# Splitting 128 tokens per partition into five tiles of two pieces, with six weight transfers on the store queue

## The chip, the cores and the metric

The kernel runs on one core of a Trainium2 chip. The metric is the device time of one execution in microseconds. A core has engines that run side by side, each with its own queue of instructions: VectorE (DVE in the profile), ScalarE (ACT), GpSimd (POOL), SyncE (SP) and TensorE, which has no work here. Transfers between the chip's main memory (HBM) and the on-chip memory (SBUF, 128 partitions) are issued by SP or ACT and carried out by 16 DMA engines.

## The reference

Every token is a row of 512 numbers and has two expert weights. The output holds each token's row twice, once times each weight; the expert indices are an input that the result does not use.

```python
batch, seq, hidden, n_experts = 16, 1024, 512, 8
k = 2
x_expanded = x[:, :, np.newaxis, :].repeat(k, axis=2)
weights = expert_weights[..., np.newaxis]
return (x_expanded * weights).astype(np.float32)
```

There are 16,384 tokens: 33.55 MB are read and 67.11 MB written, in float32.

## The kernel before

The tokens are laid over the 128 partitions, so each partition has 128 of them ("128 tokens" below means 128 per partition). They are worked through in five tiles of 25 and a rest of 3 (`groups`, `LAST`). In a tile, partition p holds 25 consecutive tokens, so that one partition's row of a load is up to 25 x 2 KB long and of a store twice that.

*Loads.* `load(i)` issues a tile's load from ACT's queue into one of two buffers of `x_pool`. The first tile comes as 9 and 16 tokens (`FIRST`). Tiles 0 and 1 are loaded ahead; after that the load of tile i + 2 is issued when tile i has been multiplied. With tile 2 the three left-over tokens are loaded into `z_tile`; a one-element copy (L76) into it ties that load to a point in ScalarE's order.

*Weights.* Three transfers on SP's queue, issued inside the first load: tile 0's weights (L97), those of tiles 1 to 4 in one strided transfer (L99), and those of the rest (L106). SP's queue also carries all stores, so these stand ahead of the first store.

*Multiplication.* `fill` gives VectorE the first `v` tokens of a piece, in operations of up to four tokens (`CH`; 4 tokens are 128x4096 elements out), and ScalarE the others, one operation for each token and weight (128x512, L119). For tiles 0 and 1 a piece has 9, 9, 9 or 8 tokens on VectorE and 4 or 3 (then 4 and 4) on ScalarE; from tile 2 on VectorE does all (`SHARES`).

*Stores.* The results go into one buffer, `o_ring`, of 25 tokens. A tile is cut into pieces at fixed places: 13 and 12 tokens in tiles 0 and 1, 9, 8 and 8 in tiles 2 to 4. Each piece is stored from SP as soon as it is filled (L154), and its place can be filled again when its store has landed. The 3-token rest is the fourteenth and last store. In the texts below 0A, 0B are the pieces of tile 0, and so on.

What sets the order is the order in which the program issues work to each engine's queue, and the waits that the framework derives from the buffers: an operation waits for the landing of what it reads and of the store that last read the place that it writes.

Of the kernel before, what the change touches and what calls it, by code (L numbers as in the profile page):

```python
# [1 line left out]

# [4 lines left out]


@with_exitstack
def kernel(  # L10
    ctx: ExitStack,
    tc: tile.TileContext,
    x: bass.AP,
    expert_indices: bass.AP,
    expert_weights: bass.AP,
    out: bass.AP,
):
    nc = tc.nc

    batch, seq, hidden = x.shape  # L20
    k = expert_weights.shape[-1]
    P = nc.NUM_PARTITIONS
    ntok = batch * seq
    assert ntok % P == 0
    A_TOTAL = ntok // P

    f32 = mybir.dt.float32
    row = k * hidden
    CH = 4


    groups = [25, 25, 25, 25, 25]
    TX = max(groups)
    LAST = 3
    FIRST = [9, 16]
    SHARES = [[9, 9], [9, 8], [9, 8, 8]]
    assert sum(groups) + LAST == A_TOTAL

    xf = x.rearrange("b s h -> (b s) h")
    of = out.rearrange("b s k h -> (b s) (k h)")  # L40
    wf = expert_weights.rearrange("b s k -> (b s) k")

    w_pool = ctx.enter_context(tc.tile_pool(name="w_pool", bufs=1))
    x_pool = ctx.enter_context(tc.tile_pool(name="x_pool", bufs=2))
    o_pool = ctx.enter_context(tc.tile_pool(name="o_pool", bufs=1))

    w_tile = w_pool.tile([P, A_TOTAL * k], f32)
    o_ring = o_pool.tile([P, TX * row], f32)

    def rows(of_all, done, T):  # L50
        return of_all[done * P : (done + T) * P, :].rearrange(
            "(p a) n -> p (a n)", a=T
        )


    if LAST:
        z_pool = ctx.enter_context(tc.tile_pool(name="z_pool", bufs=1))
        z_tile = z_pool.tile([P, LAST * hidden], f32)

    tiles = []  # L60
    done = 0
    for n in groups:
        tiles.append((done, n))
        done += n

    loaded = []

    def load(i):
        if i >= len(tiles):
            return  # L70
        done, n = tiles[i]
        x_tile = x_pool.tile([P, TX * hidden], f32)
        src = rows(xf, done, n)
        steps = FIRST if i == 0 else [n]
        if i == 2 and LAST:
            nc.scalar.copy(out=z_tile[:, :1], in_=o_ring[:, TX * row - 1 :])  # L76
        for e, step in enumerate(steps):
            at = sum(steps[:e])
            nc.scalar.dma_start(  # L79
                out=x_tile[:, at * hidden : (at + step) * hidden],  # L80
                in_=src[:, at * hidden : (at + step) * hidden],
            )
            if i == 0 and e == 0:
                for g in range(3):
                    weights(g)
        if i == 2 and LAST:
            nc.scalar.dma_start(out=z_tile, in_=rows(xf, A_TOTAL - LAST, LAST))
        loaded.append(x_tile)


    T0 = groups[0]
    G = len([n for n in groups[1:] if n == T0])
    head = (1 + G) * T0

    def weights(e):
        if e == 0:
            nc.sync.dma_start(out=w_tile[:, : T0 * k], in_=rows(wf, 0, T0))  # L97
        elif e == 1:
            nc.sync.dma_start(  # L99
                out=w_tile[:, T0 * k : head * k].rearrange("p (g n) -> p g n", g=G),  # L100
                in_=wf[T0 * P : head * P, :].rearrange(
                    "(g p a) n -> p g (a n)", g=G, p=P
                ),
            )
        else:
            nc.sync.dma_start(  # L106
                out=w_tile[:, head * k :], in_=rows(wf, head, A_TOTAL - head)
            )

    def product(engine, o_tile, t, x_in, c, m):  # L110

        o = t * row
        if engine is not None:
            for e in range(m * k):
                out_e = o_tile[:, o + e * hidden : o + (e + 1) * hidden]
                in_e = x_in[:, e // k * hidden : (e // k + 1) * hidden]
                w_e = w_tile[:, c + e : c + e + 1]
                if engine is nc.scalar or engine is nc.any and (c + e) % 3 == 2:
                    nc.scalar.mul(out=out_e, in_=in_e, mul=w_e)  # L119
                else:  # L120
                    nc.vector.tensor_scalar(
                        out=out_e,
                        in0=in_e,
                        scalar1=w_e,
                        scalar2=None,
                        op0=mybir.AluOpType.mult,
                    )
            return
        nc.vector.tensor_tensor(  # L129
            out=o_tile[:, o : o + m * row].rearrange(  # L130
                "p (t k h) -> p t k h", t=m, k=k
            ),
            in0=x_in[:, : m * hidden]
            .rearrange("p (t h) -> p t h", t=m)
            .unsqueeze(2)
            .to_broadcast([P, m, k, hidden]),
            in1=w_tile[:, c : c + m * k]
            .rearrange("p (t k) -> p t k", t=m)
            .unsqueeze(3)
            .to_broadcast([P, m, k, hidden]),  # L140
            op=mybir.AluOpType.mult,
        )

    def fill(o_tile, x_in, c, m, v):
        for t in range(0, v, CH):
            u = min(t + CH, v)
            product(None, o_tile, t, x_in[:, t * hidden : u * hidden], c + t * k, u - t)
        product(nc.scalar, o_tile, v, x_in[:, v * hidden :], c + v * k, m - v)

    def emit(src, dst, c, cuts, shares):  # L150
        for at, to, v in zip(cuts, cuts[1:], shares):
            o_tile = o_ring[:, at * row : to * row]
            fill(o_tile, src[:, at * hidden : to * hidden], c + at * k, to - at, v)
            nc.sync.dma_start(out=dst[:, at * row : to * row], in_=o_tile)  # L154

    for i in range(2):
        load(i)
    for i, (done, n) in enumerate(tiles):
        cuts = [0, 13, n] if i < 2 else [0, 9, 17, n]
        emit(loaded[i], rows(of, done, n), done * k, cuts, SHARES[min(i, 2)])  # L160
        load(i + 2)
    emit(
        z_tile,
        rows(of, A_TOTAL - LAST, LAST),
        (A_TOTAL - LAST) * k,
        [0, LAST],
        [LAST],
    )

# [1 line left out]
_INS = ['x', 'expert_indices', 'expert_weights']  # L171
_OUTS = [((16, 1024, 2, 512), 'float32')]


# [23 lines left out]
```

## Time and profile before

| what | value |
|---|---|
| median of 3 runs | 241.03 us (239.64 to 241.2) |
| profiled execution | 239.66 us |
| its span in the profile | 237.9 us |
| VectorE busy | 123.8 us (52%) |
| ScalarE busy | 20.2 us (8%) |
| moved by DMA | 100.80 MB, mean 424 GB/s |

The span runs from the first instruction to the last end that the profiler recorded; the device time of the same execution is 1.8 us longer. The DMA rows of the profile give the busy share of the 16 DMA engines in slices of the span. "Landing" is the time from the issue of a transfer to its completion. SPq and ACTq are the instructions by which SP and ACT issue transfers; queue q1 carries what SP issues and q10 what ACT issues.

### The profile page before, as it was taken

Reading aid. Unit: us, or ns where it says so; the run is one execution under the profiler, and the core shown is the slowest. Engines: PE = TensorE matmul, PEld = TensorE weight load, DVE = VectorE, ACT = ScalarE, POOL = GpSimd, SP = SyncE. Lnnn points to the kernel's source line nnn. Section 1 sums busy time; section 2 is a strip of 40 time slices with the busy share of each in tenths; the row PEclk is TensorE's granted clock in tenths of the full one; section 3 lists DMA queues with packets and bytes.
Section 4 is the critical chain, followed back from the end, with each engine's and each line's share of the span. In section 5 each row is a group of like instructions: output and inputs, shape, how many; then the busy total and the mean of one; then the engine's idle time right before and its main releaser. Section 6 shows DMA issues by size and latency. Waiting matters only on the chain.

```text
span 237.9 us, 167 instructions
## 1 busy us (share of the span) xinstructions
DVE 123.8 (52%) x33; ACT 20.2 (8%) x32; POOL 0.2 (0%) x4
## 2 busy tenths in 40 slices
DVE  0499800000059293089505999493096999865000
ACT  0008900000052160000000000000000000000000
POOL 0000000000000000000000000000000000000000
DMA  7999999999999999999999999899999999999996
GB/s 259 450 422 467 467 433 415 415 391 450 439 397 397 417 430 438 496 446 407 403 419 426 484 419 474 364 452 452 439 409 430 413 435 436 477 398 441 441 441 265
DMA packets 3840, 100.80 MB, mean 424 GB/s; under 512 B 1152, under 2 KB 1152, under 8 KB 1280
## 3 DMA queue, kind: packets, MB, share of 16 engines
q1 hardware_dynamic: 2832, 67.24, 65.7%
q10 hardware_dynamic: 1008, 33.55, 33.2%
HBM read 33.69 MB, written 67.11 MB: 424 GB/s over the span
## 4 chain that ended last, share of the span: by engine, by line
DMA 68%; DVE 18%; ACT 3%; issue 2%; ACTq 0%; DVEq 0%; SPq 0%
DMA out_dram<-o_ring 60%; DVE o_ring L129 18%; DMA x_tile<-in_x_dram 7%; ACT o_ring L119 2%; ACT L119 1%; ACTq L79 0%; DVEq L129 0%; SPq L154 0%; ACTq L119 0%
## 5 line engine op out<-in xcount | busy, mean ns | idle before, releaser
L129 DVE TENSOR_TENSOR o_ring<-x_tile,w_tile 128x4096 f32<-128x4096 f32 (+1 forms) x32 | 120.4, 3820 | 91.6 <-DMA out_dram<-o_ring 69.8
L119 ACT ACTIVATE o_ring<-x_tile,w_tile 128x512 f32<-128x512 f32 x30 | 18.7, 708 | 48.1 <-DMA out_dram<-o_ring 48.0
L129 DVE TENSOR_TENSOR o_ring<-z_tile,w_tile 128x3072 f32<-128x3072 f32 x1 | 3.4, 3360 | 2.1 <-DMA out_dram<-o_ring 2.1
L119 ACT ACT_TABLE_LOAD x1 | 1.3, 1283 | 19.0 <-DMA x_tile<-in_x_dram 19.0
L76 ACT COPY z_tile<-o_ring 128x1 f32<-128x1 f32 x1 | 0.2, 191 | 0.0
L182 POOL MEMSET const-bfloat16-1.0<- 128x1 bf16 x1 | 0.1, 102 | 0.0
L182 POOL MEMSET const-uint8-127<- 128x1 uint8 x1 | 0.1, 102 | 0.0
L182 POOL MEMSET const-float32-0.0<- 128x1 f32 x1 | 0.1, 99 | 0.2 <-issue 0.2
L182 POOL MEMSET const-float32-1.0<- 128x1 f32 x1 | 0.1, 99 | 0.0
## 6 DMA issues: line engine op xcount, KB each, us to landing
x_tile<-in_x_dram ACTq DMA_DIRECT2D x4, 6400.0 KB, 30.5
out_dram<-o_ring SPq DMA_DIRECT2D x6, 4096.0 KB, 21.5
out_dram<-o_ring SPq DMA_DIRECT2D x3, 4608.0 KB, 26.8
out_dram<-o_ring SPq DMA_DIRECT2D x2, 6656.0 KB, 33.1
out_dram<-o_ring SPq DMA_DIRECT2D x2, 6144.0 KB, 44.8
x_tile<-in_x_dram ACTq DMA_DIRECT2D x1, 4096.0 KB, 17.8
x_tile<-in_x_dram ACTq DMA_DIRECT2D x1, 2304.0 KB, 8.3
out_dram<-o_ring SPq DMA_DIRECT2D x1, 1536.0 KB, 19.5
```

The lines of the kernel that those rows point to most:

```text
L76: nc.scalar.copy(out=z_tile[:, :1], in_=o_ring[:, TX * row - 1 :])
L119: nc.scalar.mul(out=out_e, in_=in_e, mul=w_e)
L129: nc.vector.tensor_tensor(out=o_tile[:, o : o + m * row].rearrange("p (t k h) -> p t k h", t=m, k=k), in0=x_in[:, : m * hidden] .rearrange ...
L182: nc = _bacc.Bacc("TRN2", target_bir_lowering=False, num_devices=1)
```

## The change

The 128 tokens become five tiles of 26, 25, 26, 25 and 26 with no rest, so `z_tile`, its load, its copy and its store are gone. Each tile has two pieces, cut at 13 tokens; the ring holds two halves of 13. There are 10 stores, of 13 tokens or, in the 25-token tiles' second piece, of 12. The two x buffers are written out as `x_even` and `x_odd`. The first tile is loaded as 9 and 17 tokens, the third as 23 and 3. The weights come in six transfers on SP: one for each of the first four tiles and two for the last, cut at 13 tokens. VectorE takes 9 tokens of each piece of tile 0 and 10 of each piece after it, in operations of 4, 4 and 1 or 2 tokens; ScalarE takes the remaining 4, 3 or 2 tokens in every tile.

In the built program, ScalarE has 16 products, then the two loads of tile 2, then 10 products of tile 1 and 2 of tile 2, the load of tile 3, and so on. The load of tile 1 waits for the landing of the first load, and the 3-token load for the landing of the fourth weight transfer.

```diff
-    groups = [25, 25, 25, 25, 25]
-    TX = max(groups)
-    LAST = 3
-    FIRST = [9, 16]
-    SHARES = [[9, 9], [9, 8], [9, 8, 8]]
-    assert sum(groups) + LAST == A_TOTAL
+    CH = 4
+    groups = [26, 25, 26, 25, 26]
+    HALF = 13
+    FIRST = 9
+    SHORT = 3
+    assert sum(groups) == A_TOTAL
...
-    o_ring = o_pool.tile([P, TX * row], f32)
+    x_even = x_pool.tile([P, groups[0] * hidden], f32)
+    x_odd = x_pool.tile([P, groups[1] * hidden], f32)
+    o_ring = o_pool.tile([P, 2 * HALF * row], f32)
...
+    def load(i, at=0, to=None):
+        if i < len(tiles):
+            part = slice(at * hidden, (to or tiles[i][1]) * hidden)
+            nc.scalar.dma_start(out=x_of(i)[:, part], in_=rows(xf, *tiles[i])[:, part])
+
+    def weights(i, *cuts):
         done, n = tiles[i]
+        for at, to in zip((0, *cuts), (*cuts, n)):
+            nc.sync.dma_start(
+                out=w_tile[:, (done + at) * k : (done + to) * k],
+                in_=rows(wf, done, n)[:, at * k : to * k],
             )
...
+    load(0, 0, FIRST)
+    for i in range(len(tiles) - 1):
+        weights(i)
+    weights(len(tiles) - 1, HALF)
+    load(0, FIRST)
+    load(1)
+    for i, (done, n) in enumerate(tiles):
+        src, dst = x_of(i), rows(of, done, n)
+        for at, to in ((0, HALF), (HALF, n)):
             o_tile = o_ring[:, at * row : to * row]
+            fill(
+                o_tile,
+                src[:, at * hidden : to * hidden],
+                (done + at) * k,
+                to - at,
+                10 if i else 9,
+            )
             nc.sync.dma_start(out=dst[:, at * row : to * row], in_=o_tile)
-    for i in range(2):
-        load(i)
-    for i, (done, n) in enumerate(tiles):
-        cuts = [0, 13, n] if i < 2 else [0, 9, 17, n]
-        emit(loaded[i], rows(of, done, n), done * k, cuts, SHARES[min(i, 2)])
-        load(i + 2)
-    emit(
-        z_tile,
-        rows(of, A_TOTAL - LAST, LAST),
-        (A_TOTAL - LAST) * k,
-        [0, LAST],
-        [LAST],
-    )
+        if i == 0:
+            load(2, 0, groups[2] - SHORT)
+            load(2, groups[2] - SHORT)
+        else:
+            load(i + 2)
```

More of the change, by code (lines that the diff above doesn't have):

```diff
@@ L43 @@
     w_pool = ctx.enter_context(tc.tile_pool(name="w_pool", bufs=1))
-    x_pool = ctx.enter_context(tc.tile_pool(name="x_pool", bufs=2))
+    x_pool = ctx.enter_context(tc.tile_pool(name="x_pool", bufs=1))
     o_pool = ctx.enter_context(tc.tile_pool(name="o_pool", bufs=1))
     w_tile = w_pool.tile([P, A_TOTAL * k], f32)
-    o_ring = o_pool.tile([P, TX * row], f32)
+    x_even = x_pool.tile([P, groups[0] * hidden], f32)
+    x_odd = x_pool.tile([P, groups[1] * hidden], f32)
+    o_ring = o_pool.tile([P, 2 * HALF * row], f32)
     def rows(of_all, done, T):
@@ L53, in rows @@
         )
-    if LAST:
-        z_pool = ctx.enter_context(tc.tile_pool(name="z_pool", bufs=1))
-        z_tile = z_pool.tile([P, LAST * hidden], f32)
     tiles = []
@@ L64 @@
         done += n
[L66 to L70, printed above, removed]
-        done, n = tiles[i]
[L72 to L81, printed above, removed]
-            )
[L83 to L88, printed above, removed]
@@ L91 @@
[L91 to L103, printed above, removed]
-            )
[L105 to L142, printed above, removed]
@@ new lines, in x_of @@
+    def x_of(i):
+        return (x_odd if i % 2 else x_even)[:, : tiles[i][1] * hidden]
+    def load(i, at=0, to=None):
[3 more added lines that the diff above has]
+    def weights(i, *cuts):
+        done, n = tiles[i]
+        for at, to in zip((0, *cuts), (*cuts, n)):
+            nc.sync.dma_start(
+                out=w_tile[:, (done + at) * k : (done + to) * k],
+                in_=rows(wf, done, n)[:, at * k : to * k],
+            )
@@ L146, in fill @@
             u = min(t + CH, v)
[L147 to L151, printed above, removed]
-            o_tile = o_ring[:, at * row : to * row]
-            fill(o_tile, src[:, at * hidden : to * hidden], c + at * k, to - at, v)
-            nc.sync.dma_start(out=dst[:, at * row : to * row], in_=o_tile)
@@ L156 @@
-    for i in range(2):
-        load(i)
-    for i, (done, n) in enumerate(tiles):
-        cuts = [0, 13, n] if i < 2 else [0, 9, 17, n]
-        emit(loaded[i], rows(of, done, n), done * k, cuts, SHARES[min(i, 2)])
-        load(i + 2)
-    emit(
-        z_tile,
-        rows(of, A_TOTAL - LAST, LAST),
-        (A_TOTAL - LAST) * k,
-        [0, LAST],
-        [LAST],
-    )
+            nc.vector.tensor_tensor(
+                out=o_tile[:, t * row : u * row].rearrange(
+                    "p (t k h) -> p t k h", t=u - t, k=k
+                ),
+                in0=x_in[:, t * hidden : u * hidden]
+                .rearrange("p (t h) -> p t h", t=u - t)
+                .unsqueeze(2)
+                .to_broadcast([P, u - t, k, hidden]),
+                in1=w_tile[:, c + t * k : c + u * k]
+                .rearrange("p (t k) -> p t k", t=u - t)
+                .unsqueeze(3)
+                .to_broadcast([P, u - t, k, hidden]),
+                op=mybir.AluOpType.mult,
+            )
@@ new lines, in fill @@
+        for e in range(v * k, m * k):
+            nc.scalar.mul(
+                out=o_tile[:, e * hidden : (e + 1) * hidden],
+                in_=x_in[:, e // k * hidden : (e // k + 1) * hidden],
+                mul=w_tile[:, c + e : c + e + 1],
+            )
+    load(0, 0, FIRST)
[7 more added lines that the diff above has]
+        for at, to in ((0, HALF), (HALF, n)):
+            o_tile = o_ring[:, at * row : to * row]
+            fill(
[4 more added lines that the diff above has]
+                10 if i else 9,
+            )
+            nc.sync.dma_start(out=dst[:, at * row : to * row], in_=o_tile)
+        if i == 0:
[3 more added lines that the diff above has]
+            load(i + 2)
```

## The prediction

> **What bounds the kernel now.** I read the page first, then busy time by stretches of the span, then the timeline, the chain of waits, the groups by shape and the transfers.
>
> ```profile
> span 237.9 us, 167 instructions
> DVE 123.8 (52%) x33; ACT 20.2 (8%) x32; POOL 0.2 (0%) x4
> DMA  7999999999999999999999999899999999999996
> DMA packets 3840, 100.80 MB, mean 424 GB/s; under 512 B 1152, under 2 KB 1152, under 8 KB 1280
> ```
>
> VectorE works half the span and ScalarE a twelfth; the DMA engines have a 9 in every slice but the first, the last and one 8. So the end is set by 100.80 MB passing through them, which the change leaves as it is: every token is still read once and written twice. The stretches show what is lost (time, three engines, clock, DMA share, GB/s; a packet seems to be booked where it starts, so a short stretch can pass 1.00 and the next falls short):
>
> ```profile
> 0.00:2.00 2.00, 0.00 (x0) 0.00 (x0) 0.20 (x4) 1.00 0.35 51
> 6.00:48.00 42.00, 19.77 (x6) 10.16 (x16) 0.00 (x0) 1.00 1.01 434
> 48.00:50.00 2.00, 0.00 (x0) 0.00 (x0) 0.00 (x0) 1.00 0.86 225
> 50.00:52.00 2.00, 0.00 (x0) 0.00 (x0) 0.00 (x0) 1.00 1.50 590
> 52.00:90.00 38.00, 17.60 (x5) 10.02 (x16) 0.00 (x0) 1.00 1.00 435
> 180.00:233.00 53.00, 32.45 (x9) 0.00 (x0) 0.00 (x0) 1.00 1.00 432
> 233.00:237.90 4.90, 0.00 (x0) 0.00 (x0) 0.00 (x0) 1.00 0.65 278
> ```
>
> I take 434 GB/s as the rate: 100.80 MB are 232.3 us of it, so of the 237.9 us some 5.6 are lost. The last 4.9 us move 1.36 MB, 3.1 us' worth: 1.8 lost. The first 2 us move 0.1 MB: 1.8 lost, with more in the ramp behind. Around 49 us there is a dip: 225 GB/s for 2 us lacks 1.0 us, of which the next row's 590 gives some back by its booking. Start and end stay; the dip may change. An edit can therefore gain about 1 us, and it can lose wherever it lets the DMA engines run dry. The question for each part is whether it does.
>
> **The change part by part.** The profiled execution took 239.66 us, 1.8 over its span; the sum goes against that. The runs shown are 239.64, 241.03 and 241.2, so with the profiled one two lie near 239.65 and two near 241.1; the mean of the four is 240.38, which is 0.72 above the profiled one.
>
> *Six weight transfers instead of three.*
>
> ```profile
> 0.72 0.37 SPq L97 DMA_DIRECT2D w_tile<-in_expert_weights_dram  x1
> 1.15 0.43 SPq L99 DMA_DIRECT2D w_tile<-in_expert_weights_dram  x1
> q1 hardware_dynamic: 376, 0.07, 3.3%
> x_tile<-in_x_dram ACTq DMA_DIRECT2D x1, 6400.0 KB, 32.6
> w_tile<-in_expert_weights_dram SPq DMA_DIRECT2D x1, 25.0 KB, 5.5
> w_tile<-in_expert_weights_dram SPq DMA_DIRECT2D x1, 3.0 KB, 50.5
> ```
>
> The last four rows are of the transfers' view for 0 to 20 us. Three more issues by 0.43 us keep SP until 3.4 us; its next work, the first store, was issued at 25.3. A transfer of 3 KB takes 50.5 us to land while the DMA engines move 434 GB/s, so the small rows wait their turn beside the loads and displace next to nothing. They are 768 rows before (128 x 1, x 4, x 1) and 768 after (6 x 128). Cost 0. Without the cover of the loads the three issues would cost 1.3 us, the upper bound; the lower is 0, as no row is saved.
>
> The Trainium skill ("DMA: Bandwidth & Descriptors", "Anatomy of one DMA") gives a fixed cost of about 2.0 us per transfer, and its "Rules for kernel authors" say that under 64 KB one pays mostly overhead; all six transfers here are below that. By it three more would add an estimated 6 us (245.7 us) if they stood on the path. The same section says that most of this cost is the wait for the last byte's receipt, which other transfers can overlap; the 434 GB/s beside a 50.5 us landing agree with that, so it stays out of the sum.
>
> *First loads, order on ScalarE.*
>
> ```profile
> 18.97 1.28 ACT L119 ACT_TABLE_LOAD   x1 [18.97 <-DMA x_tile<-in_x_dram]
> 20.27 8.68 ACT L119 ACTIVATE o_ring<-x_tile,w_tile 128x512 f32<-128x512 f32 x14
> 29.05 0.34 ACTq L79 DMA_DIRECT2D x_tile<-in_x_dram  x1
> ```
>
> Tile 0 has 26 tokens, so its second load (17 tokens) lands 0.6 us later (0.262 MB), and ScalarE has 16 products of 0.62 us instead of 14. The third tile's load is issued at 18.97 + 0.6 + 1.28 + 9.92 = 30.8 us, not 29.05. Load 1 landed at 1.6 + 32.6 = 34.2, then 34.8: the load queue has 4.0 us in hand, before 5.2. In the built program load 1 also waits for the very first load to land (VectorE starts on that at 9.05 us); the 17 tokens, issued ahead of it, occupy the engines until about 19. The 3-token load waits for the fourth weight transfer's landing; behind it on ScalarE stand only products of tile 1, which wait for store 0A until 67 us anyway. Cost 0. If the load queue did run dry, store 0A, issued at about 26, would fill in: order, not time.
>
> *The loads ahead of the first store.* It carries 77 tokens of loads instead of 78. The old 3-token load lies in the dip, where its 6 KB rows meet the last small weight rows; the new 3-token load has the same 6 KB rows and meets weight rows of 104 B. I take the dip as unchanged; bounds -1.0 (gone) to +1.0 (doubled).
>
> *Two pieces of the ring instead of three.* This is the part that could hurt: one half is stored while the other is filled, and no third piece waits in the queue. How long a fill takes:
>
> ```profile
> 25.30 42.41 DMA out_dram<-o_ring
> 67.83 9.91 DVE o_ring L129 x3
> 77.80 13.27 DMA out_dram<-o_ring
> 82.23 5.01 ACT L119 ACTIVATE o_ring<-x_tile,w_tile 128x512 f32<-128x512 f32 x8 [9.40 <-DMA out_dram<-o_ring]
> L129 DVE TENSOR_TENSOR o_ring<-x_tile,w_tile 128x1024 f32<-128x1024 f32 x6 | 7.3, 1218 | 0.0
> L129 DVE TENSOR_TENSOR o_ring<-z_tile,w_tile 128x3072 f32<-128x3072 f32 x1 | 3.4, 3360 | 2.1 <-DMA out_dram<-o_ring 2.1
> 81.00:83.00 2.00, 0.70 (x1) 0.77 (x2) 0.00 (x0) 1.00 0.99 426
> ```
>
> Store 0A lands at 67.72 and 1A is issued at 77.80: 10.08 us with 9 tokens on VectorE. After, 10 tokens: the last operation has 2048 elements, which the trace does not show; between 1218 and 3360 ns I take the midpoint, 2.29 us, so 1.07 more and 11.15 us. ScalarE's at most 6 products (4.3 us by the 8.68 for 14) lie beside it. Store 0B lands at 82.23, when ScalarE goes on: 14.51 us after 0A, as 6.29 MB at 434 GB/s should. So store 1A was issued 4.43 us before its predecessor landed, and the row of 81 to 83 us has 0.99 of the engines busy: 4.43 us are enough. How few would do is bounded below by the start: the first issue at 0.72 has bytes moving before 2.0 us, so about 1.3.
>
> After, the half in flight is 13 tokens, 15.7 us, against a fill of 11.15: 4.55 us in hand, at four hand-overs with no queue behind them (1A, 2B with load 4, 3B, 4B). One is tighter: store 3B has 12 tokens, 14.5 us, so 4A is issued 3.35 us before it lands, 1.1 less than was tested. Its cost lies between 0 (if 1.3 us are enough) and 1.1 (if it takes all of 4.43). The middle, 2.9, is below 3.35: I take 0.
>
> As landing times: 0A 67.1, 0B 82.8, then 1A, 1B and load 3 (19.66 MB) by 128, 2A, 2B and load 4 (20.45 MB) by 175, 3A 190.9, 3B 205.4, 4A 221.1, 4B 236.8. The loads land long before their tiles come (load 4 by 175, its first fill at 191). The end is where it was.
>
> *Ten stores instead of fourteen.* 512 fewer rows of data, 13 tokens each and not 3 to 13, and 64 fewer completions: 576 small steps, 36 per engine. From above a step costs what a small packet takes in the row of queue 1 (3.3% of 20 us on 16 engines over 376 packets): 28 ns, so 1.0 us. From below 0; 435 and 432 GB/s with large and with small store rows lean to a gain, but lie within the booking's noise. I take -0.3.
>
> Sum: 239.66 + 0 + 0 + 0 + 0 - 0.3 = 239.36 us for an execution like the profiled one, and with the 0.72 by which executions lie above it on the mean, **240.1 us**: no change within about 1% (2.4 us), which is what a measurement of this kernel can tell from none.
>
> **The rivals.**
> *The hand-overs run dry (slower).* If a store must be issued L us before its predecessor lands, the ring loses 4 x (L - 4.55) + (L - 3.35) us, counting positive terms. It decides from L = 5.1: then 4.0 us, 244.1 with the 0.72. For it: two pieces instead of three, and the longest landing of a store is 53.2 us in a crowded queue. Against it: no loss at 4.43. Only if the fill is also slower than I work out does it come about.
>
> ```profile
> out_dram<-o_ring SPq DMA_DIRECT2D x1, 6144.0 KB, 53.2
> ```
>
> *Small rows are dear (faster).* If a packet costs the 28 ns and the dip goes, because the new 3-token load is issued late and runs beside store rows of 53 KB, the gain is 1.0 + 1.0: 237.7 for the profiled kind, 1.4% below the median. For it: the dip stands just where 6 KB and small rows meet. Against: as many small rows are left, and 590 GB/s follows the dip.
>
> *The weight transfers come onto the path.* 1.3 us, 241.4: for it, the fourth weight transfer now releases a load; against, its landing is needed by no operation before 67 us.
>
> *The change does not hold the first store back.* The small rows could be through the queue early, with store 0A mixing with the third load. That moves landings, not bytes: still 240.1.
>
> **How the numbers follow.** Hand-overs 0.09, small rows 0.12, weights 0.05, no holding back 0.06, the forecast 0.68. Faster by over 1% is the second rival and 0.02 of the forecast, for executions that stay near 239.4: 0.14. Slower by over 1% is the first: 0.09. Within 1%: 0.77. The range goes down to 239.36 - 0.9 = 238.5 (most of the dip or of the packets) and up to 241.2 + 1.1 = 242.3 (the slower execution with the tight hand-over's full price).
>
> **What would show it.** In the changed kernel's profile: 9s in all DMA slices but the ends; 10 tokens on VectorE in 11.1 us from landing to store issue; store 0A landing near 67 us, 4A issued near 202; load 3 issued near 94 (before 91.1). Stretches under 420 GB/s at 204 to 206 us would mean that the two-piece ring runs dry, and a bare gap between 31 and 36 us that the third load comes late. A DMA digit below 9 in the middle, or a longer last stretch, makes the forecast wrong.

## The result, and the profile after

The changed kernel takes 242.19 us (median of 6 runs, 241.76 to 243.91), the kernel before 239.92 us beside it (6 runs). The ratio is 1.0104, with a 95% interval of 1.0071 to 1.0137: slower by 1%. The forecast was "no change", 240.1 us. The profiled execution took 241.89 us. Medians here and below count every run, while a ratio leaves out runs more than 1.5% above the fastest of their kernel.

From the page of the changed kernel (span, busy time, DMA slices, GB/s by slice, queues):

```profile
span 240.1 us, 193 instructions
...
DVE 107.5 (45%) x30; ACT 39.0 (16%) x61; POOL 0.2 (0%) x4
...
DMA  7999999999999999999999999999999999999993
GB/s 269 446 425 435 453 451 393 392 404 426 426 452 426 444 452 452 419 420 407 437 477 433 426 435 427 426 426 426 426 426 435 439 459 426 425 426 426 426 426 151
...
q14 instruction: 1, 0.01, 0.0%
```

The middle is as full as forecast: 9s throughout. The span is 2.2 us longer, and the only slice that looks worse is the last one, a 3 where the kernel before has a 6. A row is new: queue 14 moved one packet of 8 KB behind the start, a fetch of instructions.

The end of the changed kernel by stretches, followed by two stretches of 0.04 us, each so short that a single packet begins in it. The columns are the stretch and its length in us, the busy time of DVE, ACT and POOL, the clock, the DMA share (of the packets that begin in the stretch) and GB/s; share x 16 engines x 0.04 us is then the time of that one packet:

```profile
234.00:236.00 2.00, 0.00 (x0) 0.00 (x0) 0.00 (x0) 1.00 0.99 426
236.00:237.00 1.00, 0.00 (x0) 0.00 (x0) 0.00 (x0) 1.00 0.13 53
237.00:240.10 3.10, 0.00 (x0) 0.00 (x0) 0.00 (x0) 1.00 0.00 0
...
144.98:145.02 0.04, 0.00 (x0) 0.00 (x0) 0.00 (x0) 1.00 3.07 1331
146.38:146.42 0.04, 0.04 (x1) 0.04 (x1) 0.00 (x0) 1.00 5.32 1331
```

From 236 to 237 us 53 GB/s begin: exactly one row of 53,248 B, on one DMA engine. By the trace's packets it begins at 236.93 and ends at 238.89, while the other 15 engines end between 236.83 and 237.17. So this kernel ends with one late engine. The two short stretches show where most of its delay comes from: the first row of load 4 takes 3.07 x 0.64 = 1.97 us on an ordinary engine and 5.32 x 0.64 = 3.40 us on the late one.

I call *spread* how far the slowest of the 16 DMA engines ends a store behind their mean, worked out from the completion packets. In the kernel before it is 0.27 us at store 0A and 0.31 at the end. In the changed kernel it is 0.31 when the first load lands, 0.72 behind the second, 1.13 at store 0A, and 2.37 behind load 4. Without its late engine it would have ended some 0.4 us behind the kernel before. Followed row by row, the late engine is the one that was last at store 0A, and it works without a gap from there to the end. So its 2.2 us are about 0.9 us from the first 68 us (1.13 less 0.27) and 1.4 us from that one row of load 4.

What happens at load 4, in the timeline of the changed kernel (start, length, engine; in brackets the idle time before and what ended it):

```profile
129.12 2.56 ACT L96 ACTIVATE o_ring<-x_even,w_tile 128x512 f32<-128x512 f32 x4 [23.91 <-DMA out_dram<-o_ring]
129.19 10.96 DVE L81 TENSOR_TENSOR o_ring<-x_even,w_tile 128x4096 f32<-128x4096 f32 x3 [16.77 <-DMA out_dram<-o_ring]
...
140.24 0.35 ACTq L68 DMA_DIRECT2D x_even<-in_x_dram  x1
146.29 3.78 ACT L96 ACTIVATE o_ring<-x_odd,w_tile 128x512 f32<-128x512 f32 x6 [14.62 <-DMA out_dram<-o_ring]
...
193.44 10.96 DVE L81 TENSOR_TENSOR o_ring<-x_even,w_tile 128x4096 f32<-128x4096 f32 x3 [4.77 <-DMA out_dram<-o_ring]
...
204.46 14.83 SPq L119 DMA_DIRECT2D out_dram<-o_ring  x2
```

Store 1B lands at 129.1, the fill of 2B takes 11 us, and at 140.2 store 2B and load 4 are issued together. The completions of store 2A, which is in flight, go out 2.6 to 4.2 us later on 15 engines and 5.7 us later on one, 3.3 on the mean. In the kernel before this *lead* was 12.4 us at load 4, where a store of 8 tokens, issued 8.7 us before the load, was still in flight, and 9.8 at load 3. In the changed kernel the lead is 3.2 us at load 3 too; there the rows are too long by only 0.05 us per engine. The last two rows show the price further on: store 3A lands on the late engine, so 4A is filled from 193.44 and issued at 204.46, not near 202. Fifteen engines stand idle for some 0.4 us before it; the late one does not.

### The profile page after: what moved, and what is told of

Same layout as the page of the kernel before. It is cut to its first block, busy times and chain, and to the rows that moved or that the text cites. A ratio compares the mean times of both kernels' runs of the same rounds, so it can differ in the third digit from the quotient of the medians.

```text
span 240.1 us, 193 instructions
## 1 busy us (share of the span) xinstructions
DVE 107.5 (45%) x30; ACT 39.0 (16%) x61; POOL 0.2 (0%) x4
## 4 chain that ended last, share of the span: by engine, by line
DMA 69%; DVE 18%; issue 2%; DVEq 2%; ACT 1%; ACTq 0%; SPq 0%
DMA out_dram<-o_ring 61%; DVE o_ring L81 18%; DMA x_even<-in_x_dram 8%; DVEq L149 2%; ACT o_ring L96 1%; ACTq L68 0%; DVEq L81 0%; SPq L119 0%
## 5 line engine op out<-in xcount | busy, mean ns | idle before, releaser
L81 DVE TENSOR_TENSOR o_ring<-x_even,w_tile 128x4096 f32<-128x4096 f32 (+2 forms) x18 | 63.6, 3590 | 41.6 <-DMA out_dram<-o_ring 31.7
L81 DVE TENSOR_TENSOR o_ring<-x_odd,w_tile 128x4096 f32<-128x4096 f32 (+1 forms) x12 | 43.8, 3709 | 69.8 <-DMA out_dram<-o_ring 63.6
L96 ACT ACTIVATE o_ring<-x_even,w_tile 128x512 f32<-128x512 f32 x40 | 25.2, 709 | 60.5 <-DMA out_dram<-o_ring 60.5
L96 ACT ACTIVATE o_ring<-x_odd,w_tile 128x512 f32<-128x512 f32 x20 | 12.7, 709 | 91.1 <-DMA out_dram<-o_ring 91.1
## 6 DMA issues: line engine op xcount, KB each, us to landing
x_even<-in_x_dram ACTq DMA_DIRECT2D x1, 4352.0 KB, 18.6
```

The costliest lines, as they stand in the source:

```text
L81: nc.vector.tensor_tensor(out=o_tile[:, t * row : u * row].rearrange("p (t k h) -> p t k h", t=u - t, k=k), in0=x_in[:, t * hidden : u * h ...
L96: nc.scalar.mul(out=o_tile[:, e * hidden : (e + 1) * hidden], in_=x_in[:, e // k * hidden : (e // k + 1) * hidden], mul=w_tile[:, c + e : ...
```

## The experiments

Times stand against the kernel before on the same chip; the ratio has its 95% interval.

**Fetch of instructions or hand-overs?** The kernel before, with 34 small operations on ScalarE:

```diff
+    spare = w_pool.tile([P, 64], f32)
...
+        if i in (1, 2):
+            for e in range(17):
+                at = i * 17 + e
+                nc.scalar.copy(out=spare[:, at : at + 1], in_=w_tile[:, e : e + 1])
```

> The kernel before with 34 more one-element copies on ScalarE (0.2 us each, into a spare tile, while ScalarE has nothing to do), so that ScalarE executes 84 profiled instructions instead of 50, as many as in the changed kernel. Theory (one DMA engine is held up by a fetch of instructions in mid-run, because ScalarE has more of them): the queue of instruction fetches shows one 8 KB packet behind the start, one DMA engine ends 1.2 to 1.4 us behind the others, span 239.2, 1.3 us over the kernel before (ratio 1.005). Rival (the two-piece ring's hand-overs are the loss, and the fetch is harmless): the fetch may appear, but the span stays at 237.9 (ratio 1.000).

Measured: 239.78 us, ratio 1.0001 (0.9989 to 1.0013). The fetch is there, at 77.5 us, and holds one engine for 0.31 us; the spread at the end is 0.24 us. The fetch comes with ScalarE's number of instructions and costs nothing here. My first theory fell.

The changed kernel, with fewer products on ScalarE:

```diff
+    ON_DVE = [[9, 9], [12, 12], [13, 12], [13, 12], [10, 12]]
-                10 if i else 9,
+                ON_DVE[i][at // HALF],
```

> The changed kernel with 28 products on ScalarE instead of 60 (VectorE takes 12 or 13 tokens of the pieces of tiles 1 to 3 and of 4B), so that ScalarE executes about 52 profiled instructions; ring, loads, weights and stores are unchanged. Theory (fetch): no 8 KB fetch in mid-run, the slowest DMA engine ends 1.1 instead of 2.4 us behind the mean, span 238.7 to 238.9, 1.2 us under the changed kernel (240.6 us). Rival (hand-overs): fills are up to 2.2 us longer, so the ring runs dry more and it is slower than the changed kernel, 243 us or more.

Measured: 244.85 us, 1.0207 (1.0193 to 1.022), as the rival had it. There is no fetch. Load 4 is issued at 144.33, when store 2A has 0.6 us left. The stretch from 2 to 10 us behind that issue:

```profile
146.33:154.33 8.00, 7.30 (x2) 0.00 (x0) 0.00 (x0) 1.00 0.93 346
```

A share of 0.93 with 346 GB/s: the engines are busy and yet move a fifth less. In the packets all 16 first rows of load 4 take 2.1 to 4.1 us instead of 1.97, and most first rows of the store 2.1 to 3.1. So this is not idleness alone; rows are slow. Behind load 3, where the lead is 1.4 us, rows are too long by another 1.2 us per engine. Idle time adds 1.1 us per engine over the run.

**Parts of the change alone.** The kernel before with six weight transfers:

```diff
-                for g in range(3):
+                for g in range(6):
                     weights(g)
...
+        at, n = tiles[e] if e < len(tiles) else (A_TOTAL - LAST, LAST)
+        nc.sync.dma_start(out=w_tile[:, at * k : (at + n) * k], in_=rows(wf, at, n))
```

> The kernel before with the weights in six transfers (one for each of the five tiles, one for the rest) instead of three; all else as before. If six transfers on the store queue throw the DMA engines out of step at the start (0.4 us in the changed kernel by 19 us), the span grows by 0.4 us to 238.3 (ratio 1.002). Rival (the second load's size or the wait of the third load does it): 237.9, ratio 1.000.

Measured: 239.89 us, 1.0006 (0.9998 to 1.0015). Six transfers cost at most 0.15%. Load 1 now waits for the first load, and the 3-token load is issued at 41.5 us: the waits of the changed kernel are all there, without harm.

The changed kernel with the third tile loaded whole:

```diff
-        if i == 0:
-            load(2, 0, groups[2] - SHORT)
-            load(2, groups[2] - SHORT)
-        else:
-            load(i + 2)
+        load(i + 2)
```

> The changed kernel with the third tile loaded whole (26 tokens) instead of as 23 and 3. Theory (the 6 KB rows beside the small weight rows cost the dip at 48 to 52 us and 0.4 us of spread between the DMA engines): no dip, 0.4 to 1.2 us less than the changed kernel, 240.7 to 241.5 us; the fetch stays. Rival (the dip belongs to the small weight rows themselves, or hidden): 241.9, as the changed kernel.

Measured: 244.17 us, 1.012 (1.0077 to 1.0163): not faster at all. The expectation failed. Its profiled execution took 247.65 us, over 3 us above the median, so no profile shows a usual execution.

The changed kernel again:

> The changed kernel itself, once more, timed and profiled beside the three below. If the slow first row of load 4 on the one DMA engine that comes to it last (3.40 us instead of 1.97 at 146.4 us) is the rule, it stands again in this profile, and that engine ends 1.9 us behind the mean; if it was an accident of one execution, the span is 238 to 239 us here.

Measured: 241.83 us, 1.0061 (1.0039 to 1.0082), runs from 240.2 to 245.4. The slow row stands again in the profile (1.53 us too long, on the engine that comes last), with a spread of 1.09 us at store 0A and 1.84 at the end. Both profiles of this kernel have it, but the total varies from run to run far more than that of the kernel before (239.4 to 240.2).

The changed kernel with three pieces in tiles 2 to 4:

```diff
-        for at, to in ((0, HALF), (HALF, n)):
+        cuts = [0, HALF, n] if i < 2 else [0, 9, 17, n]
+        for at, to in zip(cuts, cuts[1:]):
...
-                10 if i else 9,
+                (10 if i else 9) if i < 2 else to - at,
```

> The changed kernel with tiles 2 to 4 cut as before, at 9 and 17 tokens, all on VectorE; loads, weights and tiles 0 and 1 stay. Theory Ring (with two pieces a load and a store are issued together with less than two store rows per engine left ahead of them, and the engine that comes to the load last pays): about 2 us less than the changed kernel, 240.2. Rival Start (the DMA engines get 0.8 us out of step by 52 us and stay so): 241.0 or more, 0.5 us of spread above that of the kernel before at the end.

Measured: 242.48 us, 1.0094 (1.0059 to 1.0129): no cure. In the profile the 3-token rows of one engine fall between the rows of the first two stores and end at 84 us instead of 52; its spread is 2.58 us by 127 us. Load 4 has a lead of 5.9 us here and still rows that are too long by 0.58 us per engine.

The kernel before with two pieces everywhere:

```diff
-    SHARES = [[9, 9], [9, 8], [9, 8, 8]]
+    SHARES = [[9, 9], [9, 8], [10, 10]]
...
-        cuts = [0, 13, n] if i < 2 else [0, 9, 17, n]
+        cuts = [0, 13, n]
```

> The kernel before with all tiles cut in two (13 and 12 tokens, 10 on VectorE and 3 or 2 on ScalarE from tile 2 on); loads, weights and the 3-token rest stay. Theory Ring: 1 to 2.5 us over the kernel before, with slow first rows of load 4. Rival Start: as before, 239.8, since nothing is changed ahead of 128 us.

Measured: 239.81 us, 1.0014 (0.9995 to 1.0033). Two pieces alone cost nothing that shows; theory Ring in that form fell. The lead at load 4 is 5.6 us here.

The changed kernel with the fetch moved forward:

```diff
+    spare = w_pool.tile([P, 64], f32)
...
             load(2, groups[2] - SHORT)
+            for e in range(30):
+                nc.scalar.copy(out=spare[:, e : e + 1], in_=w_tile[:, e : e + 1])
```

> The changed kernel with 30 one-element copies on ScalarE behind the two loads of tile 2 (at about 41 us, while ScalarE is idle), so that the 8 KB fetch of instructions falls before 90 us and not on the start of load 4 at 147 us. If the fetch at that moment is what holds up the slow row, the row is 1.97 us and the time 240.5 us; if not, 242 us as the changed kernel.

Measured: 241.15 us, 1.0049 (1.0031 to 1.0068), against 1.0061 for the changed kernel on the same chip: the intervals overlap. The fetch lies at 72 us, and the profile has no slow row, but the spread was small too (0.52 us at store 0A) and the lead 4.6 us, and the profiled execution took 240.15 us, 1.0 below the median. Inconclusive on the row, and no cure for the time.

**Tile sizes.** The changed kernel with 25-token tiles, and with one tile of 26 (the edit is the list of groups; the small last tile is stored in one piece):

```diff
-    groups = [26, 25, 26, 25, 26]
+    groups = [25, 25, 25, 25, 25, 3]   # then [26, 25, 25, 25, 25, 2], [25, 25, 26, 25, 25, 2], [25, 25, 25, 25, 26, 2]
```

> The changed kernel with tiles of 25, 25, 25, 25, 25 and 3 tokens instead of 26, 25, 26, 25, 26 (third one loaded as 22 and 3, weights in six transfers, two pieces of 13 and 12, the 3-token tile loaded when tile 3 is read and stored last). Theory Size (tiles of 26 tokens put the DMA engines out of step or slow the first rows of their loads; the ring, the six weight transfers and the waits are harmless, as the kernel before with each of them alone showed): 239.8 to 240.2 us, ratio 1.000 to 1.002. Rival Split (the 3-token load cut out of a tile, 6 KB rows 50 KB apart, does it): 241 us or more.

> As the kernel with tiles of 25 and a small last one, but the first tile has 26 tokens (loaded as 9 and 17) and the last 2. Theory Size, if the first tile decides: spread of the DMA engines over the mean of 0.7 us or more by 19 us and 241 us; if another tile does: as the kernel with tiles of 25.

> As the kernel with tiles of 25 and a small last one, but the third tile has 26 tokens (loaded as 23 and 3) and the last 2. If this tile decides: 241 us, with spread that grows at 47 to 52 us; if not: as the kernel with tiles of 25.

> As the kernel with tiles of 25 and a small last one, but the fifth tile has 26 tokens and the last 2. If load 4 with its 53 KB rows decides (the row of 3.40 us in the changed kernel): 241 us, with such a row near 146 us; if not: as the kernel with tiles of 25.

Measured: 243.38 us and 1.0138 (1.0099 to 1.0177); 241.19 and 1.0058 (1.0036 to 1.008); 242.29 and 1.0109 (1.0091 to 1.0127); 242.57 and 1.0126 (1.0107 to 1.0145). Tiles of 25 are no cure by themselves, so theory Size fell as the whole story, and the other three cannot single out a tile. The profile of the first shows something else, in the stretch from 2 to 10 us behind load 4:

```profile
139.23:147.23 8.00, 3.75 (x1) 3.79 (x6) 0.00 (x0) 1.00 0.99 378
```

Again rows are slow, with a lead of 4.0 us.

**The lead.** I then worked out, for load 4 of each trace, how long the store in flight still lasted on the mean of the engines, and by how much all rows that began in the next 12 us were too long, per engine:

| kernel | lead, us | rows too long, us per engine |
|---|---|---|
| before | 12.4 | 0.00 |
| changed, three pieces | 5.9 | 0.58 |
| before, two pieces | 5.6 | 0.03 |
| changed, early fetch | 4.6 | 0.01 |
| changed, tiles of 25, third of 26 | 4.2 | 0.96 |
| changed, tiles of 25 | 4.0 | 0.91 |
| changed | 3.3 | 0.11 (1.44 on one engine) |
| changed, load 3 | 3.2 | 0.05 |
| changed, tiles of 25, fifth of 26 | 2.8 | 0.77 |
| changed, fewer on ScalarE | 0.6 | 1.62 |

The lead orders the rows only roughly: 5.9 us did not save the kernel with three pieces, and load 3 of the changed kernel got by with 3.2. Three more runs test it, and a fourth the dip near 49 us. The changed kernel with shorter fills:

```diff
-                10 if i else 9,
+                8 if i else 9,
```

> The changed kernel with 8 instead of 10 tokens on VectorE in the pieces of tiles 1 to 4 (ScalarE 5 or 4): a fill takes 9.1 us instead of 11.3. Theory Lead (a load that is issued together with a store slows its and the store's first rows when the store in flight ends less than some 4.5 us after the issue): the lead at load 4 grows from 3.3 to 5 us or more, no slow first row, no idle time near 205 us, span 238 to 238.5, 240.0 to 240.3 us. Rival (the fetch of instructions or the spread from the start decide): 241.5 to 242.5, as the changed kernel.

Measured: 240.63 us, 1.0049 (1.0027 to 1.0071). The lead is 7.8 us, the rows are too long by 0.06, no idle time at 205 us, span 238.7. Its page, and then its timeline on ScalarE:

```profile
span 238.7 us, 215 instructions
...
DMA  7999999999999999999999999999999999999994
```

```profile
128.73 5.01 ACT L96 ACTIVATE o_ring<-x_even,w_tile 128x512 f32<-128x512 f32 x8 [19.54 <-DMA out_dram<-o_ring]
137.65 0.35 ACTq L68 DMA_DIRECT2D x_even<-in_x_dram  x1
148.29 6.24 ACT L96 ACTIVATE o_ring<-x_odd,w_tile 128x512 f32<-128x512 f32 x10 [14.55 <-DMA out_dram<-o_ring]
```

From landing (128.73) to issue (137.65) it is 9 us instead of 11, and the store in flight lands at 148.29, 10.6 us behind the issue. Hardly a slow row and no idle time are left in this profile, and the median is 0.3 us above the expected range. By the times alone the gain is not certain: the interval reaches into those of the changed kernel (1.0039 to 1.0082 and 1.0071 to 1.0137), which did not run beside it.

The changed kernel with loads 3 and 4 held back:

```diff
+            if 1 < i < len(tiles) - 1 and at == 0:
+                nc.scalar.copy(out=x_of(i + 1)[:, :1], in_=o_tile[:, HALF * row - 1 :])
+                load(i + 1)
         if i == 0:
...
-        else:
-            load(i + 2)
```

> The changed kernel with loads 3 and 4 held back by a one-element copy until the first piece of the tile before is filled, so that each is issued alone, some 10 us ahead of the end of the store in flight; the fills stay at 11.3 us. Theory Lead: no slow first rows, 240.0 to 240.6 us (the tight hand-over to 4A may stay). Rival (length of the fills, whatever is issued with the stores): 241.5 to 242.5.

Measured: 240.65 us, 1.004 (1.0021 to 1.006); load 4 is issued alone at 148.3, 18.6 us ahead of the end of the store in flight, and the rows are too long by 0.01. The fills are as long as in the changed kernel, so in this execution their length alone makes no row slow; that points to how little is left in flight when the load is issued. It is not settled: the profiled execution took 240.04 us, 0.6 below the median, and the interval overlaps the lower one of the changed kernel.

The kernel before with two pieces and longer fills:

```diff
-    SHARES = [[9, 9], [9, 8], [9, 8, 8]]
+    SHARES = [[9, 9], [9, 8], [12, 12]]
...
-        cuts = [0, 13, n] if i < 2 else [0, 9, 17, n]
+        cuts = [0, 13, n]
```

> The kernel before with all tiles cut in two, as in the earlier run, but 12 tokens on VectorE in the pieces of tiles 2 to 4, so that a fill takes 13.3 us instead of 11.1 and the lead at load 4 falls by 2.2 us, to 2 to 3.4. Theory Lead: slow first rows of load 4, 0.8 to 1.5 us per engine, 241 us or more, though fetch, start and loads are those of the kernel before. Rival (start or tile sizes): 239.8 to 240.3.

Measured: 242.81 us, 1.0118 (1.01 to 1.0136), where the same kernel with short fills had 1.0014. The lead is 1.8 us and the rows are too long by 1.08 us. From 2 to 10 us behind its load 4:

```profile
142.72:150.72 8.00, 7.45 (x2) 1.33 (x2) 0.00 (x0) 1.00 0.93 358
...
187.00:189.00 2.00, 1.91 (x1) 0.00 (x0) 0.00 (x0) 1.00 0.31 133
```

So a loss of this size can be made in the kernel before, with its start, weights and tiles untouched. The slow rows are the smaller part of it. The longer fills also leave the engines idle ahead of stores 3B and 4A, at 188 and 204 us (the second row shows the former), by the packets 1.0 us per engine each time. These 2.1 us are hand-overs that run dry.

The kernel before with the 3-token load moved behind load 4:

```diff
-        if i == 2 and LAST:
+        if i == 4 and LAST:
```

> The kernel before with its 3-token load issued behind load 4 instead of behind load 2, so that no 6 KB rows meet small weight rows. If the dip at 48 to 51 us belongs to that meeting: 0.6 to 0.8 us less than the kernel before, ratio 0.997. If it is of the weight rows themselves: 1.000. Store 0A may start to mix with the weights; that costs nothing by the prediction's steps.

Measured: 239.94 us, 1.0012 (1.0001 to 1.0022). No gain: the 6 KB rows are gone from the dip, but now the last rows of load 2 take 0.83 us per engine too long at 46 to 49 us. In both kernels the loss sits where the small weight rows run out, beside whichever load is there.

**What is left over.** Both cures together, and the fast fill with tiles of 25:

```diff
-    groups = [26, 25, 26, 25, 26]
+    groups = [25, 25, 25, 25, 25, 3]
...
-                10 if i else 9,
+                min(to - at, 8 if i else 9),
```

> Tiles of 25, 25, 25, 25, 25 and 3 tokens in two pieces, as in the earlier run with them (1.0138), but with 8 instead of 10 tokens on VectorE from tile 1 on. Theory Lead: the lead grows by some 2 us, the slow rows go, 239.8 to 240.4 us. If what is left over in the changed kernel with the fast fill (0.4 to 0.5%) belongs to the tiles of 26 tokens, this one comes to 239.8 to 240.0 (ratio 1.000 to 1.001); if it belongs to the 3-token load cut out of a tile, to 240.5.

> The changed kernel with both cures, 8 tokens on VectorE and loads 3 and 4 held back. If the 0.4 to 0.5% left over with each cure alone is still of the lead, the ratio goes to 1.000 to 1.002; if it stems from the first 52 us (the spread of the DMA engines there), it stays at 1.003 to 1.005.

Measured: with tiles of 25 and the fast fill 239.8 us, 1.0003 (0.9994 to 1.0012). Both cures with tiles of 26: 240.65 us, 1.0034 (1.0022 to 1.0046). The page of the former, and its timeline on ScalarE:

```profile
span 237.9 us, 214 instructions
...
DMA  7999989899999999999999999999999999999996
```

```profile
134.81 0.35 ACTq L68 DMA_DIRECT2D x_even<-in_x_dram  x1
145.32 5.01 ACT L96 ACTIVATE o_ring<-x_odd,w_tile 128x512 f32<-128x512 f32 x8 [14.41 <-DMA out_dram<-o_ring]
```

Load 4 goes out at 134.81, and the store in flight is landed at 145.32 on the slowest engine, 10.5 us behind it, against 6.05 in the changed kernel (140.24 to 146.29). The last slice is a 6 again, and the span that of the kernel before, with six weight transfers, a cut-out 3-token load, two pieces and the fetch all in place. The loss has two parts, then. With tiles of 25, the fills alone decide between 1.0138 and 1.0003. With the fast fill, the tiles alone decide between 1.0049 (three of 26) and 1.0003 (25 and a small last one). Both cures with tiles of 26 leave 1.0034, and in that profile it is spread: the last store lands at 236.76 on the mean of the engines, as in the kernel before (236.78), but 1.27 us later on the slowest.

## Why the prediction was wrong

*The failed step is the two-piece ring.* I reckoned with a hand-over from one store to the next, found 4.43 us enough in the kernel before, and counted the end of tile 2 as one of "four hand-overs" with 4.55 us in hand. (1B, issued with load 3, is a fifth that the list left out.) The cost was put at 0; at load 4 it was 1.44 us on the engine that ended last. Two things were wrong. The tested hand-over was a store alone. At the end of a tile a load goes out with the store, and for that the kernel before has no test below 9.8 us, so I should have bounded it. In every trace the first row of load 3 or 4 comes 3.2 to 4.4 us after its issue, and in most cases rows were slow where the store in flight ended about then or sooner. And I measured "in hand" from landing to landing, which is the slowest engine's time. On the mean engine some 0.3 us of landing and 1.1 us of spread come off it: 3.3 us were left, not 4.55.

*The 16 DMA engines are not one.* The sum held bytes against a rate, and on the mean of the engines that was right: the stores landed at 82.7 (0B), 128.0 (1B), 175.2 (2B), 191.0 (3A) and 205.5 us (3B), where I had 82.8, 128, 175, 190.9 and 205.4. The last one landed 0.6 us later than in the kernel before, idle time included. What grew is the spread, from 0.3 to 1.9 us at the end, which no term stood for; 0.9 us of it was there at store 0A, ahead of any hand-over in the ring. I had said that order moves landings and not time; but a late engine makes a landing late, which makes the next fill late, which shortens the lead.

*The rival "hand-overs run dry" had the right place and sign.* Its price formula did not fit: it counted idle engines alone, and here the ring's loss on the late engine came as one slow row. In the kernel before with longer fills, idle engines were the larger part. The tight hand-over to 4A, which I took at 0, lost some 0.4 us on 15 engines, because store 3A landed at 193.3 instead of 190.9. My sign for it, under 420 GB/s at 204 to 206 us, did not show it, since a packet is booked where it starts:

```profile
204.00:206.00 2.00, 0.40 (x1) 0.00 (x0) 0.00 (x0) 1.00 1.00 424
```

The store issued at 204.46 has its first row at 205.29 on an empty queue, 0.84 us later. From these 0.84 us and the 0.3 us of landing I estimate that 3.35 us would have been ample; the end is set by the late engine, which has no gap there. The Trainium skill ("DMA: Bandwidth & Descriptors", "Latency and other measured facts") gives about 0.6 us to the first byte for this kind of transfer; the lone store's 0.84 us is near it, the loads' 3.2 to 4.4 us beside a store are not.

*Luck, and a term without a source.* 242.19 us lies just inside the range, but that is luck: its upper end was 241.2 us plus 1.1 us for the hand-over to 4A, and the loss came from elsewhere. The 0.72 us added to the sum rests on the runs of 241.03 and 241.2 us. In 105 later runs of the kernel before (239.41 to 240.64 us, median 239.73) none like them came again. Against the sum without it, 239.36 us, the miss is 2.8 us.

*Right:* the weights (cost 0; measured 1.0006), the waits of load 1 and of the 3-token load, the fill (11.15 us forecast; 129.1 to 140.2 measured), load 3 at 94.9 (forecast 94), a full middle, and the dip as unchanged (rows of 6 KB too long by some 0.8 us per engine before, 0.95 after). Not shown: the gain of 0.3 us from fewer rows; the kernel before with 11 stores has 1.0014 and no gain. The 2.0 us per transfer from the Trainium skill ("DMA: Bandwidth & Descriptors", "Anatomy of one DMA") stand in a section on transfers issued from GpSimd; these are issued from SP, so the 245.7 us were a loose estimate.

*Still open:* why tiles of 26 tokens keep 0.34%, and what makes the first rows slow. The profiles with a first tile of 26 have spreads of 0.5 to 1.1 us at store 0A; those with 25 have 0.27 to 0.54. That goes with the time left over, but nothing here shows its cause.

## What to carry to other kernels

When a kernel is bound by transfers, look for the last slices of the DMA row and ask whether all engines end together; a span can grow with every byte rate unchanged. When a change takes pieces out of a ring, work out for each load how much of the store in flight is left at the moment when load and next store are issued, counted on the mean of the engines and not on the slowest landing. Over loads 3 and 4 of all traces here, leads of 7.8 us or more cost at most 0.08 us per engine, leads of 3 to 6 us went either way (0.01 to 0.96), and every lead under 3 us cost 0.17 us or more. A part that is harmless alone (two pieces: 1.0014) can be costly with another (two pieces and longer fills: 1.0118), so test it with the margins of the kernel it goes into.

## What was not expected of the hardware

A load that is issued while a store is in flight waits 3.2 to 4.4 us for its first row, also when no store is issued with it (3.7 and 4.4 us with the loads held back), while a store alone on an empty queue waits 0.84 us. Where the store in flight runs out in between, the first rows of load and store took up to 4.1 us instead of 1.97, with 0.93 to 0.99 of the engines' time busy.

A store's completion can wait behind a load's row: on one engine of the changed kernel, load 4's row came at 144.00 just before the completion of store 2A, which went out at 145.97, so the landing shows at 146.29. The Trainium skill ("DMA: Bandwidth & Descriptors", "Queues, rings and completion order") says that an engine takes turns between queues packet by packet, and the trace agrees; a packet is here a whole row of up to 53,248 B.

ScalarE's program was fetched in mid-run, one packet of 8 KB, in every kernel with 80 or more profiled ScalarE instructions, and in none with 59 or fewer. It held one engine for 0.31 us and cost nothing (1.0001). The Trainium skill ("Runtime: NRT & Kernel Launch", "Instruction fetch mechanics") speaks of blocks of 16 KiB and a cost that is mostly hidden; the block is 8 KB here, and hidden it is.
